# GLA score matmuls of a pair's two heads alternated in the two row groups of the array

## The chip, the cores and the metric

The kernel runs on one core of one Trainium2 chip. The metric is the device time of one execution in microseconds; a kernel's time is the median of its timed runs. The core has a matrix engine (TensorE, in the rows PE for its matmuls and PEld for its weight loads), VectorE (DVE), ScalarE (ACT), GpSimd (POOL) and SyncE (SP), which issues most of the loads. Each engine works through its own list of instructions in order.

## The reference, cut to what matters

The reference is one step of a diffusion trunk of two layers over 128 context tokens and 128 latent tokens, width 2048. Each layer has three mixers side by side (gated linear attention, softmax attention and DeltaNet) and an MLP. The change lies in the gated linear attention (GLA): 4 heads, key width 64, value width 128, run once forward and once backward over the tokens. Within a chunk its scores are

```python
b = jnp.cumsum(gc, axis=-2)
diff = b[..., :, None, :] - b[..., None, :, :]
dec = jnp.where(mask, jnp.exp(jnp.where(mask, diff, 0.0)), 0.0)
A = jnp.einsum('bhid,bhijd,bhjd->bhij', qc, dec, kc)
o = jnp.einsum('bhij,bhjv->bhiv', A, vc) + jnp.einsum('bhid,bhdv->bhiv', qc * jnp.exp(b), S)
```

so that each score is a sum over the 64 key channels of q, k and a decay between the two tokens, with the gate different in each channel.

## The kernel before, in words

All matmuls of the layers go through `mm` (line 85). Most of TensorE's work is a stream of projections and MLP products: a weight block is loaded by SyncE, split on ScalarE into a high part (`hi`) and on VectorE into a low part (`lo`), and multiplied with the activations (`g` and `gt` in the rows). `mod` are the products of the modulation.

The decay of GLA can't be pulled out of one product for all token pairs, so the kernel works in levels. For each level, a block size of 64, 32, 16, 8, 4, 2 or 1 tokens, queries and keys are scaled by the decay to the middle of their block (`scaled`: tiles `tq` and `tk_`, seven levels each). One product of 128 by 128 per level gives the scores of token pairs whose halves differ at that level, and a mask picks them. An eighth product, of the unscaled q and k, gives the diagonal. A token group `g` (0 context, 1 latent) and a column `c` hold a pair of heads: the tile has 128 partitions, the first head in partitions 0 to 63 and the second in 64 to 127. There are 4 pairs per layer and 8 in the kernel.

`intra(g, c, hh)` makes the scores of one head. It contracts over 64 partitions only, and `tile_position=(64 * hh, 0)` places the product in the upper or the lower half of the array's rows. The eight products go to two PSUM banks of the pool `pm` (three banks, used by the other steps of this chain too; `ga` in the rows): the diagonal and three levels in the first, four levels in the second, each bank with an order token of its own, so that within a bank the products are issued in this order. The diagonal is copied to the tile `AT` by ScalarE with a factor of 2, and then VectorE copies the seven levels into `AT` under their masks (COPY_PREDICATED in the rows). A bank can be given to a new tile when the last of its readers is done. `outs` multiplies `AT` with the values (`obg`).

`gla_chain` is a generator: it yields between its steps (decay, scaling, the scores of the first head, of the second, outs, stats). `weave` runs this chain, the two softmax chains (`att_chain`) and a normalisation together with a filler, which holds the remaining projections of the layer and the modulation. It keeps a clock of TensorE's assumed time; when no chain is due yet, it takes a piece of the filler. A chain is due again after `K0 + K1 *` the assumed time of its VectorE and ScalarE work (0.4 and 0.7). From the order that results, the framework's scheduler then fixes each engine's list at build time with a simulated timeline, and may move instructions against each other where data and order tokens allow.

The lines that the rows name: 85 is `mm`, 94 `tp`, 55 every VectorE and ScalarE instruction.

Of the kernel before, what the change touches and what calls it, by code (L numbers as in the profile page):

```python
# [12 lines left out]
I32 = mybir.dt.int32  # L13
AF = mybir.ActivationFunctionType
# [26 lines left out]
def tile_hybrid_step(ctx: ExitStack, tc: tile.TileContext, A: dict, O: dict):  # L41
# [17 lines left out]
    ve, se = Timed(nc.vector, 1 / 960, 0.13), Timed(nc.scalar, 1 / 1400, 0.27)  # L59

    def pool(name, bufs=1, **kw):
        return tc.tile_pool(name=name, bufs=bufs, **kw)
# [10 lines left out]
    pm = ctx.enter_context(pool("pm", 3, space=PS))  # L73
# [6 lines left out]
    def newtok():  # L80
        ntok[0] += 1
        return f"tok{ntok[0]}"

    def mm(out, lhsT, rhs, start=True, stop=True, tok=None, **kw):
        i = nc.tensor.matmul(out, lhsT=lhsT, rhs=rhs, start=start, stop=stop, **kw)  # L85
        n = math.prod(rhs.shape[1:])
        pe_t[0] += max(n / 2400 * (1 if rhs.dtype == F32R else 4), 0.027)
        if tok is not None:
            tc.stamp_issue_order_token(i.ins, tok)
        return i  # L90
# [21 lines left out]
    gmask = cp.tile([P, 7, P], F32, tag="c_gmask", name="gmask")  # L112
# [526 lines left out]
    for l in range(L):  # L639
        modc, s12, _, _ = mods[l]  # L640
# [23 lines left out]
        if l > 0:  # L664
            lay = open_layer(l)
        lctx, dnc, reg, sml, o_dn, gqk, gv, aq, akv, misc, dqk, vt = [
            lay[k] for k in ("lctx", "dnc", "reg", "sml", "o_dn", "gqk", "gv", "aq", "akv", "misc", "dqk", "vt")
        ]
# [184 lines left out]
        def pbank(nm, pp):  # L853
            t = pp.tile([P, 512], F32, tag="m", name=nm)
            return t.rearrange("p (h c) -> p h c", h=4)
# [39 lines left out]
        def dn_group(g):  # L895
            pp = (pm, pn)[g]

            def tr(nm, tag="tr", bufs=3):
                return dp.tile([P, 4, P], F32, tag=f"{tag}{g}", name=nm, bufs=bufs)
# [104 lines left out]
            for d in range(2):  # L1004
                yield
                vsrc = vt[:, g].rearrange("p (h v) -> p h v", h=4)
                if g == 1:
                    kb = bank("kb")
                    for h in range(4):
                        mm(kb[:, h], dqk[:, 4 + h, gs], s0d[:, d, h])  # L1010
                    R = tr("R")
                    for h in range(4):
                        ve.scalar_tensor_tensor(
                            R[:, h], kb[:, h], nec[:, d * 4 + h : d * 4 + h + 1], vsrc[:, h], ALU.mult, ALU.add
                        )
                else:
                    R = vsrc
                if g == 1:
                    yield
                vb = bank("vb")  # L1020
                for h in range(4):
                    mm(vb[:, h], N[d][:, h], R[:, h])
                v_ = tr("vn", "vn", 2)
# [80 lines left out]
        def gla_chain():  # L1104
# [4 lines left out]
            tq = gp.tile([P, 7, P], F32, tag="tq", name="tq")  # L1109
            tk_ = gp.tile([P, 7, P], F32, tag="tk", name="tk")  # L1110
            qi = gp.tile([P, 2, 2, P], F32, tag="qi", name="qi")
            ks = gp.tile([P, 2, 2, P], F32, tag="ks", name="ks")
            AT = gp.tile([P, 8, P], F32, tag="AT", name="AT")

            def decay(g, c, d):
                if c == 0 and d == 0:
                    lah = gp.tile([P, 512], F32R, tag="lah", name="lah")
                    lal = gp.tile([P, 512], F32R, tag="lal", name="lal")
                    se.activation(lah, t12[:, g], AF.Copy, scale=1.0 / 16.0)
                    ve.scalar_tensor_tensor(lal, t12[:, g], 1.0 / 16.0, lah.bitcast(F32), ALU.mult, ALU.subtract)  # L1120
                    lahl[:] = [lah, lal]
                lah, lal = lahl
                off = 0 if g == 0 else P
                e = gp.tile([P, 8, P], F32, tag="e", name="e", bufs=2)
                for b2 in range(2):
                    eb = pm.tile([P, 512], F32, tag="m", name="eb")
                    ls = slice(d * 256 + c * P, d * 256 + c * P + P)
                    rs_ = wr[d][:, off + b2 * 512 : off + b2 * 512 + 512]
                    mm(eb, lah[:, ls], rs_, start=True, stop=False)
                    mm(eb, lal[:, ls], rs_, start=False, stop=True)  # L1130
                    se.activation(e[:, 4 * b2 : 4 * b2 + 4].rearrange("p a b -> p (a b)"), eb, AF.Exp)
                return e

            def scaled(g, c, d, e):
                lb = 1 if g == 0 else 0
                q_ = gqk[:, c, g * P : g * P + P]
                k_ = gqk[:, 2 + c, g * P : g * P + P]
                for li, s in enumerate(GLEV):
                    ev = e[:, lb + li].rearrange("p (b h s) -> p b h s", h=2, s=s)
                    qv = q_.rearrange("p (b h s) -> p b h s", h=2, s=s)  # L1140
                    kv = k_.rearrange("p (b h s) -> p b h s", h=2, s=s)
                    tqv = tq[:, li].rearrange("p (b h s) -> p b h s", h=2, s=s)
                    tkv = tk_[:, li].rearrange("p (b h s) -> p b h s", h=2, s=s)
                    ve.tensor_tensor(tqv[:, :, 1 - d], qv[:, :, 1 - d], ev[:, :, 1 - d], ALU.mult)
                    ve.tensor_tensor(tkv[:, :, d], kv[:, :, d], ev[:, :, d], ALU.mult)
                if g == 0:
                    ve.tensor_tensor(ks[:, d, c], k_, e[:, 0], ALU.mult)
                else:
                    ve.tensor_tensor(qi[:, d, c], q_, e[:, 7], ALU.mult)

            def intra(g, c, hh):
                R = slice(64 * hh, 64 * hh + 64)
                i8 = g * 4 + c * 2 + hh
                tk0, tk1 = newtok(), newtok()
                b0 = pbank("ga0", pm)
                b1 = pbank("ga1", pm)
                gsl = slice(g * P, g * P + P)
                mm(b0[:, 0], gqk[R, 2 + c, gsl], gqk[R, c, gsl], tok=tk0, tile_position=(64 * hh, 0))
                for li in range(7):
                    o_ = (b0 if li < 3 else b1)[:, (li + 1) % 4]  # L1160
                    tt = tk0 if li < 3 else tk1
                    mm(o_, tk_[R, li], tq[R, li], tok=tt, tile_position=(64 * hh, 0))
                se.activation(AT[:, i8], b0[:, 0], AF.Copy, scale=2.0)
                for li in range(7):
                    src = (b0 if li < 3 else b1)[:, (li + 1) % 4]
                    ve.copy_predicated(AT[:, i8], gmask[:, li].bitcast(I32), src)

            def outs(g):
                gs = slice(g * P, g * P + P)
                ob = pbank("obg", pm)  # L1170
                tk = newtok()
                for h in range(4):
                    mm(ob[:, h], gv[:, g, h * P : h * P + P], AT[:, g * 4 + h], start=True, stop=(g == 0), tok=tk)
                    if g == 1:
                        for d in range(2):
                            mm(ob[:, h], s0g[0][:, d, h], qi[:, d, h // 2], start=False, stop=(d == 1), tok=tk)
                se.activation(o_gl[:, :, gs], ob, AF.Copy)
                sq = gp.tile([P, 4, P], F32, tag="tr", name="gsq", bufs=2)
                se.activation(sq, ob, AF.Square)
                return sq  # L1180

            def stats(g, sq):
                sb_ = pm.tile([P, 512], F32, tag="m", name="stgb")
                for h in range(4):
                    mm(sb_[:, h : h + 1], sq[:, h], ones[:, 0:1])
                ve.tensor_copy(stg[0].rearrange("p (h g) -> p h g", g=2)[:, :, g], sb_[:, 0:4])
# [4 lines left out]
            for i, (g, c, d) in enumerate(steps):  # L1191
                yield
                if i < 7:
                    es[i + 1] = decay(*steps[i + 1])
                    if i == 4:
                        s0g.append(rgl.tile([P, 2, 4, P], F32, tag="t12", name="s0g"))
                        nc.gpsimd.dma_start(s0g[0], A["s0_gla"][l])
                    yield
                scaled(g, c, d, es.pop(i))
                if d == 1:  # L1200
                    for hh in range(2):
                        yield
                        intra(g, c, hh)
                    if c == 1:
                        yield
                        sq = outs(g)
                        yield
                        stats(g, sq)
# [144 lines left out]
        wo = A["w_out"][l]  # L1353
        oatt = [att_chain(0), att_chain(1)]
        weave([gla_chain(), out_norm(ap, o_dn, sto, "od", TB, lay["rs16"][:, 0:8], pn)] + oatt, filler)
        while "end" not in marks:
            next(filler, None)
# [283 lines left out]
```

## Time and profile before

| | |
|---|---|
| time, median of 3 runs | 2603.95 us (2598.66 to 2604.85) |
| span of the profiled execution, first to last instruction | 2594.0 us |
| instructions in it | 47700 |
| TensorE matmul busy | 2526.2 us, 97% |
| VectorE busy | 1804.8 us, 70% |
| ScalarE busy | 1225.7 us, 47% |
| loaded from HBM | 602.41 MB |

The profiled execution is shown by its span; the page has no time for what lies before the first and after the last instruction. Matmul records overlap, since matmuls are pipelined: a record's length is not the time that it takes from the stream. That time is read from one record's start to the next one's. An fp32 product appears as two passes, that is two weight loads and two matmuls.

### The profile page before, as it was taken

To read this page: it belongs to the slowest core of one execution; us is meant where nothing else is said; L and a number is where in the kernel's file an instruction comes from. 1 tells how busy PE (TensorE), PEld (TensorE's weight loads), DVE (VectorE), ACT (ScalarE), POOL (GpSimd) and SP (SyncE) were. 2 spreads that over 40 slices of the span, in tenths; PEclk is the share of its full clock that TensorE was granted. 3 is DMA by queue.
4 is the path that set the end of the run, shared out by engine and by line. 5 is a ranking of instruction groups with operands and counts; after the bars stand their busy time and mean duration, and the time that the engine had idled before them with its cause. 6 is when DMAs were issued, how large, how long until landed. Compare 5 with 4: busy or idle time off the path is not lost. (4 is left out here: it accounts for less than half of the span.)

```text
span 2594.0 us, 47700 instructions
## 1 busy us (share of the span) xinstructions
PE 2526.2 (97%) x18988; PEld 2257.6 (87%) x18988; DVE 1804.8 (70%) x3197; ACT 1225.7 (47%) x1925; POOL 98.2 (4%) x121
## 2 busy tenths in 40 slices
PE   6999999999999999999999999999999999999999
PEld 4777678699988999999999888898999989999888
DVE  4457758558878767776766776786789865564665
ACT  3356244446454354344355653455565435445433
POOL 1000000003000000000002100000210000000000
PEclk9999999999999999999999999999999999999999
DMA  9966767776888877888876764435578766565664
GB/s 361 330 246 215 270 217 253 274 262 199 313 300 303 292 268 266 281 292 288 279 246 227 255 217 123 144 119 169 170 229 304 259 187 188 187 190 186 185 198 142
DMA packets 169551, 611.83 MB, mean 236 GB/s; under 512 B 19744, under 2 KB 20320, under 8 KB 169328
## 3 DMA queue, kind: packets, MB, share of 16 engines
q1 hardware_dynamic: 165024, 598.94, 68.3%
q0 software_dynamic: 2432, 6.61, 0.7%
q8 instruction: 149, 2.44, 0.4%
q10 hardware_dynamic: 1872, 3.23, 0.4%
q14 instruction: 74, 0.61, 0.1%
HBM read 602.41 MB, written 6.29 MB: 235 GB/s over the span
## 5 line engine op out<-in xcount | busy, mean ns | idle before, releaser
L55 ACT ACTIVATE hi<-raw 128x1024 fp32r<-128x1024 f32 (+1 forms) x742 | 784.4, 1057 | 1080.7 <-PE g L85 574.6
L55 DVE TENSOR_TENSOR lo<-raw,hi 128x1024 fp32r<-128x1024 f32 (+1 forms) x742 | 899.2, 1218 | 342.2 <-ACT hi L55 324.9
L85 PE MATMUL g<-act,hi 128*128 128x256 f32 (+1 forms) x7488 | 1055.5, 291 | 17.2 <-ACT hi L55 6.2
L85 PEld LDWEIGHTS g<-act,hi 128*128 128x128 f32 x7488 | 954.2, 189 | 98.5 <-issue 28.9
L85 PE MATMUL g<-act,lo 128*128 128x256 f32 x4000 | 561.3, 282 | 5.6 <-DVE lo L55 5.3
L85 PEld LDWEIGHTS g<-act,lo 128*128 128x128 f32 x4000 | 513.6, 189 | 19.6 <-DVE lo L55 9.5
L55 DVE SCALAR_TENSOR_TENSOR acc<-raw,sc,acc 128x1024 f32<-128x1024 f32 x240 | 299.1, 1280 | 130.6 <-DMA raw<-w_mod 128.0
L85 PE MATMUL g<-hid,hi 128*128 128x256 f32 (+1 forms) x1536 | 262.4, 319 | 2.1 <-DVE x L55 2.1
L55 DVE SCALAR_TENSOR_TENSOR x<-g,modc,x 128x128 f32<-128x128 f32 x448 | 142.0, 347 | 170.5 <-PE g L85 165.9
L85 PEld LDWEIGHTS g<-hid,hi 128*128 128x128 f32 x1536 | 217.2, 188 | 28.2 <-ACT hi L55 5.0
L85 PE MATMUL mod<-raw,sc 128*32 128x512 f32 (+1 forms) x1280 | 154.7, 526 | 20.5 <-DMA raw<-w_mod 18.7
L85 PE MATMUL gt<-hi,act 128*128 128x512 f32 x512 | 141.6, 409 | 3.3 <-ACT hi L55 3.3
L85 PE MATMUL g<-hid,lo 128*128 128x256 f32 x1024 | 142.1, 281 | 0.0
L85 PEld LDWEIGHTS g<-hid,lo 128*128 128x128 f32 x1024 | 134.7, 188 | 6.3 <-issue 0.8
L85 PEld LDWEIGHTS gt<-hi,act 128*128 128x128 f32 x512 | 93.9, 190 | 39.5 <-issue 11.3
L492 POOL TENSOR_TENSOR ht<-x,rstd 128x256 f32<-128x256 f32 x48 | 55.6, 1177 | 1011.5 <-ACT rstd L55 1008.1
L85 PEld LDWEIGHTS mod<-raw,sc 128*32 128x32 f32 x1280 | 30.9, 109 | 59.6 <-issue 13.8
L85 PE MATMUL gt<-lo,act 128*128 128x512 f32 x256 | 75.7, 403 | 0.0
L85 PE MATMUL gl<-hid,hi 128*128 128x258 f32 x384 | 70.4, 285 | 2.1 <-ACT hi L55 2.1
L85 PEld LDWEIGHTS gl<-hid,hi 128*128 128x128 f32 x384 | 59.3, 189 | 2.6 <-ACT hi L55 2.5
L85 PEld LDWEIGHTS gt<-lo,act 128*128 128x128 f32 x256 | 47.2, 188 | 12.6 <-issue 1.1
L85 PE MATMUL gl<-hid,lo 128*128 128x258 f32 x192 | 54.1, 284 | 0.7 <-DVE lo L55 0.6
(353 smaller groups left out, 1919.3 us busy)
## 6 DMA issues: line engine op xcount, KB each, us to landing
raw<-w_ff SPq DMA_DIRECT2D x512, 512.0 KB, 4.5
raw<-w_mod SPq DMA_DIRECT2D x384, 512.0 KB, 5.2
raw<-w_in SPq DMA_DIRECT2D x86, 512.0 KB, 4.2
raw<-w_tok SPq DMA_DIRECT2D x64, 512.0 KB, 4.4
raw<-w_out SPq DMA_DIRECT2D x64, 512.0 KB, 4.1
raw<-w_in SPq DMA_DIRECT2D x16, 448.0 KB, 6.1
x<-xT SPq DMA_DIRECT2D x8, 512.0 KB, 7.3
spill<-x ACTq DMA_DIRECT2D x4, 512.0 KB, 4.2
```

The source lines that it names most:

```text
L55: return f(out, *a, **kw)
L85: i = nc.tensor.matmul(out, lhsT=lhsT, rhs=rhs, start=start, stop=stop, **kw)
L492: nc.gpsimd.tensor_tensor(t, X["x"][:, k, :], rstd, ALU.mult)
```

## The change

`intra` now takes a pair of heads. It works in two parts of four products per head: first the diagonal and levels 0 to 2, then levels 3 to 6. In a part each head has a bank of its own, and the products of the two heads alternate level by level under one order token: first head in the upper rows, second head in the lower rows, next level. After a part's products come the copies of both heads, and then a `yield`; the caller yields once ahead of the first part. The number of products, their shapes and the copies stay as they are. Before, a head's eight products were written one after the other, with a `yield` ahead of each head; there are now three of them per pair (one ahead, one behind each part) in place of two.

```diff
@@ -1148,22 +1148,27 @@
                 else:
                     ve.tensor_tensor(qi[:, d, c], q_, e[:, 7], ALU.mult)
 
-            def intra(g, c, hh):
-                R = slice(64 * hh, 64 * hh + 64)
-                i8 = g * 4 + c * 2 + hh
-                tk0, tk1 = newtok(), newtok()
-                b0 = pbank("ga0", pm)
-                b1 = pbank("ga1", pm)
+            def intra(g, c):
                 gsl = slice(g * P, g * P + P)
-                mm(b0[:, 0], gqk[R, 2 + c, gsl], gqk[R, c, gsl], tok=tk0, tile_position=(64 * hh, 0))
-                for li in range(7):
-                    o_ = (b0 if li < 3 else b1)[:, (li + 1) % 4]
-                    tt = tk0 if li < 3 else tk1
-                    mm(o_, tk_[R, li], tq[R, li], tok=tt, tile_position=(64 * hh, 0))
-                se.activation(AT[:, i8], b0[:, 0], AF.Copy, scale=2.0)
-                for li in range(7):
-                    src = (b0 if li < 3 else b1)[:, (li + 1) % 4]
-                    ve.copy_predicated(AT[:, i8], gmask[:, li].bitcast(I32), src)
+                i8 = g * 4 + c * 2
+                rows = [slice(64 * hh, 64 * hh + 64) for hh in range(2)]
+                for part in range(2):
+                    banks = [pbank(f"ga{part}", pm) for _ in range(2)]
+                    tk = newtok()
+                    for b in range(4):
+                        li = 4 * part + b - 1
+                        for hh, R in enumerate(rows):
+                            if li < 0:
+                                kk, qq = gqk[R, 2 + c, gsl], gqk[R, c, gsl]
+                            else:
+                                kk, qq = tk_[R, li], tq[R, li]
+                            mm(banks[hh][:, b], kk, qq, tok=tk, tile_position=(64 * hh, 0))
+                    for hh in range(2):
+                        if part == 0:
+                            se.activation(AT[:, i8 + hh], banks[hh][:, 0], AF.Copy, scale=2.0)
+                        for b in range(1 if part == 0 else 0, 4):
+                            ve.copy_predicated(AT[:, i8 + hh], gmask[:, 4 * part + b - 1].bitcast(I32), banks[hh][:, b])
+                    yield
 
             def outs(g):
                 gs = slice(g * P, g * P + P)
@@ -1198,9 +1203,8 @@
                     yield
                 scaled(g, c, d, es.pop(i))
                 if d == 1:
-                    for hh in range(2):
-                        yield
-                        intra(g, c, hh)
+                    yield
+                    yield from intra(g, c)
                     if c == 1:
                         yield
                         sq = outs(g)
```

## Rows read from the trace of the kernel before

**Rows 1.** The page's part 1: busy us, share of the span, instructions.

```profile
PE 2526.2 (97%) x18988; PEld 2257.6 (87%) x18988; DVE 1804.8 (70%) x3197; ACT 1225.7 (47%) x1925; POOL 98.2 (4%) x121
```

**Rows 2.** Waits of TensorE, whole span: us in total, times, longest us.

```profile
PE mod L85 <- DMA raw<-w_mod: 18.7, 8, 12.6
...
```

**Rows 3.** The same in 365 to 500 us, and in 1640 to 1775 us.

```profile
PE g L85 <- DVE x L55: 1.2, 1, 1.2
...
PE ptb L94 <- DVE p L55: 3.0, 1, 3.0
...
```

**Rows 4.** By window: length, busy of PE, PEld, DVE, ACT, POOL, clock, DMA share, GB/s.

```profile
365.00:500.00 135.00, 133.84 (x938) 96.78 (x937) 101.14 (x335) 59.93 (x116) 4.34 (x8) 1.00 0.73 255
1640.00:1775.00 135.00, 129.73 (x889) 113.45 (x887) 105.64 (x325) 67.55 (x122) 3.82 (x7) 0.99 0.38 123
390.00:410.00 20.00, 20.00 (x160) 16.26 (x159) 19.76 (x63) 7.04 (x13) 1.65 (x3) 1.00 0.80 291
1684.00:1711.00 27.00, 27.00 (x224) 26.15 (x223) 27.00 (x86) 14.47 (x25) 0.55 (x1) 1.00 0.40 122
1711.00:1730.00 19.00, 19.00 (x146) 17.36 (x144) 13.21 (x46) 9.02 (x15) 0.00 (x0) 1.00 0.45 143
```

**Rows 5.** Instructions on tile ga, whole span: ns min/median/max, first and last start.

```profile
L85 PE MATMUL ga<-tq,tk x224: 272/272/373, 371.9 to 1732.4; 64*128 64x128 f32 x112
...
L55 DVE COPY_PREDICATED AT<-gmask,ga x112: 270/296/311, 375.3 to 1737.4; 128x128 f32<-128x128 int32 x112
...
L85 PE MATMUL ga<-gqk x32: 272/322/373, 371.5 to 1730.8; 64*128 64x128 f32 x32
```

**Rows 6.** Timeline of TensorE (start us, us, instruction), bursts of one head.

```profile
371.54 0.48 PE L85 MATMUL ga<-gqk 64*128 64x128 f32 x2
...
381.81 1.33 PE L85 MATMUL g<-act,hi 128*128 128x256 f32 x10
383.07 1.16 PE L85 MATMUL ga<-tq,tk 64*128 64x128 f32 x8
384.15 0.51 PE L85 MATMUL eb<-wr,lah 128*128 128x512 f32 x1
384.50 0.39 PE L85 MATMUL eb<-wr,lal 128*128 128x512 f32 x1
...
1730.62 0.48 PE L85 MATMUL ga<-gqk 64*128 64x128 f32 x2
1730.95 1.72 PE L85 MATMUL ga<-tq,tk 64*128 64x128 f32 x14
```

**Rows 7.** Timeline of TensorE, 459 to 461.2 us.

```profile
459.84 0.37 PE L85 MATMUL ga<-tq,tk 64*128 64x128 f32 x1
459.85 0.37 PE L85 MATMUL ga<-gqk 64*128 64x128 f32 x1
460.05 0.27 PE L85 MATMUL ga<-tq,tk 64*128 64x128 f32 x1
460.06 0.27 PE L85 MATMUL ga<-gqk 64*128 64x128 f32 x1
460.16 0.84 PE L85 MATMUL ga<-tq,tk 64*128 64x128 f32 x8
460.93 0.51 PE L85 MATMUL g<-act,hi 128*128 128x256 f32 x2
```

**Rows 8.** Timeline of TensorE, 434 to 446 us.

```profile
437.05 0.71 PE L85 MATMUL ga<-tq,tk 64*128 64x128 f32 x4
```

**Rows 9.** Timeline of ScalarE and VectorE, the first and fourth readers of a bank.

```profile
372.74 0.28 ACT L55 ACTIVATE AT<-ga 128x128 f32<-128x128 f32 x1 [0.67 <-PE ga L85]
...
378.15 0.29 DVE L55 COPY_PREDICATED AT<-gmask,ga 128x128 f32<-128x128 int32 x1
```

**Rows 10.** Timeline of VectorE; in brackets idle us before it and its releaser.

```profile
486.37 0.69 DVE L55 TENSOR_TENSOR o_gl<-o_gl,bcb 128x512 f32<-128x512 f32 x1 [3.45 <-PE bcb L85]
...
1729.75 0.30 DVE L55 COPY_PREDICATED AT<-gmask,ga 128x128 f32<-128x128 int32 x1 [3.13 <-PE ga L85]
```

## The prediction, made before the change was run

> **What bounds the kernel now.** I read the page's busy line first: TensorE's matmuls are busy for 97% of the span, VectorE 70%, ScalarE 47% [rows 1]. A busy matmul row does not prove that the engine never waits, so the second view is the list of waits, for TensorE alone. Over the whole kernel its largest entry is 18.7 us, for weights of the modulation [rows 2]. In the two stretches of the change (the gated linear attention, one per layer, 365 to 500 us and 1640 to 1775 us) the list has one entry in the first, 1.2 us, and in the second 3.0 us for the softmax's p and three entries of under 1 us, all at the stretches' ends [rows 3]. So TensorE's instruction stream is what sets the end there: other matmuls (the filler) stand between the attention's own steps and cover their latency. The third view is the table by window: VectorE has 101 us of work in the first 135 us and 106 in the second, but between 1684 and 1711 us it has no idle time left (27.00 of 27.00), and between 390 and 410 us hardly any (19.76 of 20); right behind the second of these it is idle for 5.8 of 19 us [rows 4]. The transfers take 0.73 and 0.38 of the DMA engines' time there. The granted clock is 1.00 and 0.99 there, that is the 2.4 GHz level [rows 4].
>
> **What the score matmuls cost now.** There are 256 passes in the trace (224 of the levels and 32 of the unscaled pair): 128 matmuls, two passes each [rows 5]. In a burst of one head passes follow each other every 0.1115 us: 14 of them take 1.72 us, less the 0.27 of the last, over 13 gaps [rows 6]. Each burst also pays for going from the full array to half of its rows and back. In the burst at 383.07 the g passes before it run every 0.117 us ((1.33 - 0.28) / 9), the last of them starts at 382.86, and the first score pass 0.21 later: 0.09 lost. The first two passes of a burst are 0.21 apart (0.48 - 0.27), 0.10 more than later ones. The last pass starts at 383.96 and what follows 0.20 later: 0.09. And that one's first record is 0.51 long where the next has 0.39: 0.11 or 0.12, I take 0.11. Together 0.39 us per burst [rows 6]. I count 28 bursts, 16 in the first layer and 12 in the second; the first is that at 371.54, the last that of 16 passes from 1730.62 [rows 6].
>
> Seven of the 28 already hold what the change wants: passes of both heads side by side. In the clearest both heads start together, at 459.84 and 459.85, go on at 460.05 and 460.06, and stay side by side until one runs out [rows 7]. That burst has 12 passes, four of them beside another, and lasts 1.09 us to the next matmul, where 12 in a row would need 0.21 + 10 x 0.1115 + 0.20 = 1.53: four passes cost nothing. Six bursts hide three passes each and one hides four, 22 in all. So the work now is (256 - 22) x 0.1115 + 28 x 0.39 = 26.1 + 10.9 = 37.0 us of TensorE.
>
> **The change part by part.** *Alternation.* A part has four levels of both heads, 16 passes, with an order token that keeps them alternating and a bank for each head, as the burst of [rows 7] has. If the heads run beside each other a part lasts as long as 8 passes of one: 8 x 0.1115 + 0.39 = 1.28 us. Eight pairs of two parts, each whole, are 16 x 1.28 = 20.5 us, a saving of 16.5. Every further break costs 0.39. Now a pair makes three bursts (8, 16 and 8 passes) where nothing breaks them, 24, and four more come from places like 437.05, where two levels run alone between other matmuls [rows 8]. I keep these four: 20 bursts, 22.1 us, a saving of 14.9. The bounds are 16.5 (16 bursts) and 11.8 (28 again, 8 x 0.39 more than 20).
>
> By the Trainium skill, TensorE: Matmul & The Clock Gate, section "Wait — 56ns, not 53.3ns?", the sequencer can need about 62 ns for each matmul and is the bound where the array needs less; two heads side by side ask for one pass every 56 ns. The rows at 459.84 hold the faster pace for eight passes only [rows 7], and no row shows it for 16. By that rule a part's 16 passes would take 0.99 us where I have 0.89, an estimate of 1.6 us more over 16 parts.
>
> *What VectorE and ScalarE do.* 112 masked copies as before [rows 5], and 16 scaled ones, of the same sizes; only their order changes (three and three, then four and four). Cost nothing, since the work is equal.
>
> *The banks.* The pool has three. Part 1 needs two, and the second of these is the first head's bank of part 0, free after one ScalarE copy and three masked copies. Before, the same release held back only the last 8 of a pair's 32 passes; now it holds back 16. What is queued behind the first matmul of part 1 on TensorE is the filler, if the planner puts it there. At the first pair the bank is read from 372.74 to 378.44 [rows 9], and the passes that wait for it run at 383.07, 0.21 behind filler that had been put in between [rows 6]. I take nothing for it; the other end is a rival below. The attention's chain itself gets longer by the four masked copies that now follow the last part, about 4 x 0.29 = 1.2 us per pair. At the first layer's end VectorE, done with its own step of this chain, has stood 3.45 us until TensorE came to the next [rows 10], so 1.2 us later costs nothing; at the second's the stretch ends with the softmax chain, whose p TensorE waits for [rows 3], not with this one.
>
> *One more step.* The generator yields once more per pair; the planner may put one more piece of filler there. It is work that has to run anyway: nothing, as long as filler is left.
>
> *What does not arrive.* Where VectorE has no idle time, TensorE cannot get ahead for good. The bursts inside the full windows are those at 1697.87 and 1699.21 (24 passes, three of them beside others: 21 x 0.1115 + 2 x 0.39 = 3.1 us, afterwards a part and a half, 1.9) and two of the same kind at 394.0 and 397.5. I give up the 1.2 us of each, 2.4 together. Ends: 0 (VectorE's 5.8 idle us behind the second window take it back) and 8.6 (the whole of the second layer's half, 7.4, and the first's 1.2).
>
> Sum: 14.9 - 2.4 = 12.5 us less. The profiled span is 2594.0 us, and 2581.5 is expected for it. The page gives no time around it; the median of the runs, 2603.95, lies 9.95 above the span, and I leave that as it is: 2603.95 - 12.5 = 2591.5 us. A change of 0.3%, 7.8 us, is what can be told from none. If every part is whole and nothing is lost it is 2587.5.
>
> **The rivals.**
> *VectorE sets the pace (no change).* The second layer's half is lost, and the first layer's loses 1.2: 7.4 - 1.2 = 6.2, so 2597.8. For it: the full window, and TensorE's wait for p at the stretch's end. Against it: at 1729.75 VectorE itself has stood 3.13 us for score matmuls [rows 10], so it had caught up before the last bursts.
>
> *Parts broken up (no change).* If the levels come one by one, as at 435.88, each pair of matmuls is a burst of its own: 2 x 0.1115 + 0.39 = 0.61 us for one level of both heads. With half of the parts so, 8 x 1.28 + 32 x 0.61 = 29.8 us, a saving of 7.2, less 2.4: 2599.2. For it: four breaks now. Against it: 22 of the 28 bursts have 6 passes or more.
>
> *The row groups do not run together (no change).* Then 256 passes in a row and 20 bursts: 28.5 + 7.8 = 36.3, 0.7 less than now: 2603.3. The rows at 459.84 speak against it.
>
> *TensorE stands for the bank (slower).* If part 1 is queued right behind part 0, with no filler between, TensorE stands until the first head's bank has been read. At the first pair its reading takes from 372.74 to 378.44, 5.7 us, because the masked copies wait in VectorE's queue behind other work [rows 9]. With half of that, 2.85 us in each of 8 pairs, 22.8 us come on top: 2603.95 - 12.5 + 22.8 = 2614.3. It decides from 12.5 / 8 = 1.6 us per pair. For it: 16 passes behind that wait and not 8, and an order that is fixed before the run. Against it: the wait exists now and costs TensorE nothing [rows 3].
>
> **How the numbers follow.** Forecast 0.66, VectorE's pace 0.11, broken parts 0.10, no overlap 0.03, bank 0.10. The forecast's own range is 2586 to 2596: 16.5 less at one end, 11.8 - 2.4 = 9.4 at the other, and 1.6 us on either side for the order of everything else, which the planner works out anew (an estimate, half of the 3.0 us that is its largest wait in the stretches now [rows 3], rounded up). The range to the other cases is 2585 to 2604: it takes in all but the bank rival and a little at either end. Faster by over 0.3% (below 2596.1): 0.62 of the forecast's 0.66, a third of VectorE's pace and a fifth of the broken parts, 0.68. Slower by over 0.3%: 0.09 from the bank rival and 0.01 for an order that falls out badly, 0.10. The rest, 0.22, is within 0.3%.
>
> **What would show it.** After: 256 score passes in about 20 bursts, 16 at least; a part of 16 passes 0.9 us from its first start to its last, two starts within 0.02 us of each other every 0.11; the time from 365 us to the end of each layer's stretch shorter by 5 to 8 us and everything behind it unchanged. The forecast is wrong if TensorE's waits list a score matmul behind an AT copy (bank), if its waits for lo or hi in the two stretches grow by more than 3 us (VectorE), or if starts within a part are 0.11 apart one by one (no overlap).

## The result, and the profile after

The kernel with the change takes 2591.5 us (median of 8 runs, 2584.8 to 2598.9) where the kernel before took 2604.4 beside it on the same chip (8 runs, 2598.7 to 2609.5): a ratio of 0.9943, 95% interval 0.9928 to 0.9958, or 15 us less (11 to 19; the two medians lie 12.9 apart). Run again beside other kernels it gave 0.9929 (0.9913 to 0.9945) and a median of 2585.0. The forecast was 2591.5 us, with a range of 2585 to 2604.

The two profiled executions can't be compared by their spans. After's is 2597.0 us, the longest of its eight runs (2598.9 us, 1.9 more than the span; 1.8 to 2.2 in the other runs). Before's, 2594.0 plus 1.9, was faster than all of the eight runs above. What hides the gain between them lies where TensorE's order is the same in both: from the end of the first layer's stretch (below) to the start of the second's it is 1046.5 us in before's profile, 1059.6 in after's and 1047.3 in a second profile of the kernel with the change (e2). Most of it is one piece of the first layer's MLP: 274.2, 283.1 and 276.7 us. So the comparison goes by stretch: from a layer's first `eb<-wr,lah` product to the first `gl<-hid` product of its MLP.

The table by window, for the first layer's stretch and the second's (columns as in rows 4; the length is the first number). The kernel before:

```profile
359.30:588.20 228.90, 227.74 (x1703) 182.53 (x1702) 156.27 (x443) 105.80 (x190) 4.34 (x8) 1.00 0.75 260
1634.70:1854.20 219.50, 214.23 (x1581) 196.60 (x1581) 165.25 (x447) 115.51 (x200) 3.82 (x7) 0.99 0.47 151
```

The kernel with the change:

```profile
362.20:587.70 225.50, 224.62 (x1704) 178.16 (x1703) 156.49 (x448) 105.53 (x190) 4.33 (x8) 1.00 0.76 264
1647.30:1856.90 209.60, 207.17 (x1581) 190.68 (x1580) 163.35 (x447) 115.00 (x200) 3.81 (x7) 1.00 0.51 158
```

The first layer's stretch is 3.4 us shorter, the second's 9.9: 13.3 together. These lengths repeat within 2 us where TensorE's order is the same. The second layer's is 219.5, 219.8 and 219.3 in three profiles that have before's order there, and 209.6, 209.6, 209.6, 209.8 and 211.4 in five that have after's; the first layer's is 229.0 and 230.3, and 225.5, 226.4 and 226.9. (The means differ by 3.4 and 9.5.)

The page's busy line after [rows 1] and the first entry of TensorE's waits [rows 2] show no other bound:

```profile
PE 2522.5 (97%) x18988; PEld 2252.9 (87%) x18988; DVE 1802.7 (69%) x3197; ACT 1225.5 (47%) x1925; POOL 98.3 (4%) x121
```

```profile
PE mod L85 <- DMA raw<-w_mod: 18.0, 8, 12.9
```

The instructions on tile ga are as many and as long as before [rows 5]:

```profile
L85 PE MATMUL ga<-tq,tk x224: 272/272/374, 375.7 to 1741.6; 64*128 64x128 f32 x112
...
L55 DVE COPY_PREDICATED AT<-gmask,ga x112: 274/297/308, 380.4 to 1749.2; 128x128 f32<-128x128 int32 x112
```

What is new is how they stand. The timeline of TensorE at the first pair (start us, us, instruction; the rows of a burst overlap where the two heads run side by side) answers to rows 6 and 7:

```profile
374.51 0.48 PE L85 MATMUL ga<-gqk 64*128 64x128 f32 x2
374.93 0.73 PE L85 MATMUL g<-act,hi 128*128 128x256 f32 x4
375.50 0.28 PE L85 MATMUL g<-act,lo 128*128 128x256 f32 x1
375.71 0.37 PE L85 MATMUL ga<-gqk 64*128 64x128 f32 x1
375.71 0.37 PE L85 MATMUL ga<-tq,tk 64*128 64x128 f32 x1
375.92 0.27 PE L85 MATMUL ga<-gqk 64*128 64x128 f32 x1
375.93 0.94 PE L85 MATMUL ga<-tq,tk 64*128 64x128 f32 x13
376.80 1.08 PE L85 MATMUL g<-act,lo 128*128 128x256 f32 x7
```

A burst is a run of score passes with no other product between them; a pass is hidden when it starts within 0.02 us of one of the other head. Here are sixteen passes from 375.71 to the last start at 376.60 (375.93 + 0.94 - 0.27): 0.89 us, eight of them hidden. But the first head's diagonal (two passes, 374.51) has gone out alone: the order that was fixed at build time puts five other products between it and its partner, which follows 1.2 us later beside the first head's first level. Why is not settled; a bank that comes free later for the second head would do it, but no run here tests that. Most pairs come as 2, 16 and 14 passes: the lone product, then the rest of part 0 with the first product of part 1, then the rest of part 1. In the whole trace I count 24 bursts and 110 hidden passes, so by the prediction's prices (256 - 110) x 0.1115 + 24 x 0.39 = 25.6 us of score work, where before by the same count has 37.0. Added up from starts, it is 25.57 where before has 37.05: 11.5 less, 5.8 in the first layer and 5.7 in the second (some tenths more or less by how the edges of a burst are counted).

TensorE's waits in the second layer's stretch (1652.5 to 1787.5 us), which answer to rows 3:

```profile
PE g L85 <- DVE x L55: 1.5, 1, 1.5
...
```

No score matmul and no `AT` copy appears there, and the wait of `ptb` for p is gone. Its place on TensorE shows what that was worth. Timeline of the kernel before (idle us and releaser in brackets):

```profile
1759.98 1.94 PE L94 MATMUL ptb<-c_ident,p 128*128 128x128 f32 x8 [2.98 <-DVE p L55]
1761.75 1.89 PE L85 MATMUL oatb<-pT,cvv 128*128 128x512 f32 x2
1763.48 1.02 PE L85 MATMUL oatb<-pT,akv 128*128 128x512 f32 x2
```

The same instructions after:

```profile
1763.49 1.04 PE L94 MATMUL ptb<-c_ident,p 128*128 128x128 f32 x8
1764.77 1.12 PE L85 MATMUL oatb<-pT,cvv 128*128 128x512 f32 x2 [0.25 <-ACT pT L55]
1765.73 1.02 PE L85 MATMUL oatb<-pT,akv 128*128 128x512 f32 x2
```

Before, TensorE stood 2.98 us, and the rows behind the wait took 3.50 us (1759.98 to 1763.48) where after they take 2.24. The window of these 3.5 us before has a granted clock of 0.51, the 1.2 GHz level; the same rows after run at 1.00 (before, then after):

```profile
1759.90:1763.40 3.50, 3.42 (x10) 2.40 (x11) 1.14 (x2) 1.19 (x2) 0.00 (x0) 0.51 0.55 207
```

```profile
1763.40:1766.60 3.20, 2.95 (x16) 1.75 (x15) 3.09 (x4) 1.52 (x3) 0.97 (x2) 1.00 0.65 184
```

The second layer's 9.9 us are thus 5.7 of score work, 3.0 of waiting and 1.3 of lower clock. In the first layer 5.8 of score work give 3.4.

### The profile page after: what moved, and what is told of

Its sections match the earlier page's. It is cut to its first block, busy times and chain, and to the rows that moved or that the text cites. A ratio compares the mean times of both kernels' runs of the same rounds, so it can differ in the third digit from the quotient of the medians.

```text
span 2597.0 us, 47711 instructions
## 1 busy us (share of the span) xinstructions
PE 2522.5 (97%) x18988; PEld 2252.9 (87%) x18988; DVE 1802.7 (69%) x3197; ACT 1225.5 (47%) x1925; POOL 98.3 (4%) x121
## 5 line engine op out<-in xcount | busy, mean ns | idle before, releaser
L85 PEld LDWEIGHTS g<-act,hi 128*128 128x128 f32 x7488 | 955.4, 189 | 101.0 <-ACT hi L55 27.4
L85 PEld LDWEIGHTS g<-act,lo 128*128 128x128 f32 x4000 | 514.1, 189 | 24.1 <-DVE lo L55 11.8
```

## The experiments

Each was timed in five rounds; ratios are to the kernel before on the same chip. "Stretches" are the first and the second layer's, from one profile each. Score work is added up from starts; passes that are not hidden x 0.1115 + bursts x 0.39 gives the same within 0.4 us, in e7 within 1.1.

| kernel | us | ratio (95%) | stretches, us | score us (bursts) |
|---|---|---|---|---|
| before | 2602 to 2605 | 1 | 229.0, 219.5 | 37.05 (28) |
| after | 2591.5 | 0.9943 (0.9928 to 0.9958) | 225.5, 209.6 | 25.57 (24) |
| e2 after again | 2585.0 | 0.9929 (0.9913 to 0.9945) | 226.4, 209.6 | 25.57 (24) |
| e1 head by head | 2609.8 | 1.0022 (1.0010 to 1.0034) | 234.1, 222.9 | 36.56 (28) |
| e3 after, scores twice | 2612.2 | 1.0029 (1.0017 to 1.0042) | 242.0, 222.1 | 39.61 (23) |
| e4 before, scores twice | 2637.1 | 1.0130 (1.0113 to 1.0148) | 256.4, 230.4 | 62.28 (20) |
| e5 after, mod token | 2590.9 | 0.9944 (0.9925 to 0.9963) | 227.9, 209.6 | 26.00 (24) |
| e6 before, mod token | 2613.0 | 1.0031 (1.0014 to 1.0048) | 234.7, 219.8 | 38.28 (29) |
| e7 head by head, mod token | 2609.1 | 1.0020 (1.0005 to 1.0034) | 232.6, 223.0 | 39.01 (31) |
| e8 one yield less | 2589.5 | 0.9946 (0.9930 to 0.9963) | 229.7, 211.4 | 25.04 (23) |
| e9 before, fewer copies | 2620.2 | 1.0055 (1.0034 to 1.0077) | 244.9, 221.7 | 38.00 (30) |
| e10 after, fewer copies | 2589.9 | 0.9945 (0.9927 to 0.9963) | 224.8, 214.9 | 25.67 (24) |
| e11 first layer only | 2599.9 | 0.9985 (0.9972 to 0.9998) | 226.9, 219.3 | 31.24 (25) |
| e12 second layer only | 2594.1 | 0.9961 (0.9945 to 0.9977) | 230.3, 209.8 | 31.38 (27) |

**e1, the alternation undone.** Parts, banks and yields stay; only the loop order within a part goes back.

```diff
-                    for b in range(4):
-                        li = 4 * part + b - 1
-                        for hh, R in enumerate(rows):
+                    for hh, R in enumerate(rows):
+                        for b in range(4):
+                            li = 4 * part + b - 1
```

> The new kernel with the alternation alone undone: same parts, banks, copies and yields, but within a part the first head's four products are written ahead of the second head's four. In TensorE's order this makes 28 bursts, and the heads meet in nine places, at three passes each. Theory (the gain is TensorE time saved by the overlap): (256 - 27) x 0.1115 + 28 x 0.39 = 36.5 us of score work against 37.0 before and 25.6 in the new kernel, so the time of the kernel before within 2 us, 2602 to 2606, some 11 us slower than the new kernel. Rival (the gain comes from the new parts, banks and yields, through the plan of everything else): as fast as the new kernel, 2590 to 2593.

The score work is as expected (36.56 us), the time is 5.7 us above before, not equal to it. So the parts, banks and yields without the alternation give no gain; the gain comes with the alternation and the order of everything else that the planner makes with it. That the heads stand in different row groups does not suffice. The timeline of e1's first burst shows where one head's four products meet the other's: the second head's diagonal (`gqk`) starts among the last passes of the first, and only those run side by side:

```profile
373.51 0.49 PE L85 MATMUL ga<-tq,tk 64*128 64x128 f32 x3
373.74 0.37 PE L85 MATMUL ga<-gqk 64*128 64x128 f32 x1
373.85 0.27 PE L85 MATMUL ga<-tq,tk 64*128 64x128 f32 x1
373.95 0.27 PE L85 MATMUL ga<-gqk 64*128 64x128 f32 x1
```

The wait for p is there, at 4.1 us, and the modulation's products in the first layer's stretch are issued in 38 pieces (runs with no other product between them) in place of 33. The 5.7 us led to e5 to e7.

**e2, the kernel with the change once more** (no edit).

> The new kernel once more, unchanged, for another profiled execution. Both theories: 2588 to 2594. In the profiled execution of the new kernel the first layer's MLP between 1073 and 1358 us took 8.9 us longer than before, with the same order of TensorE's instructions. Theory (chance of that execution): here that piece is within 3 us of the kernel before. Rival (the changed stretch moves the loads of what follows and the MLP pays): 7 to 10 us longer again.

The stretches repeat within 1 us; the MLP piece that was 8.9 us longer in after's first profile is 2.45 longer here. That difference belongs to the execution, not to the change. The median, 2585.0 us, lies below the 2588 to 2594 that both theories had.

**e3 and e4, each score product issued twice** (the second into the same place, so nothing else changes in the data).

```diff
+                        t_ = pe_t[0]
+                        for hh, R in enumerate(rows):
...
+                            mm(banks[hh][:, b], kk, qq, tok=tk, tile_position=(64 * hh, 0))
+                        pe_t[0] = t_
```

> The new kernel with each pair of products of a level issued twice, alternating, the second time over the first (same results, copies and waits; the planner's clock does not count the second). 256 passes more. Theory (heads run side by side, and each us of TensorE in these stretches is a us of time): 128 x 0.1115 = 14.3 us more, less one burst, 0.4: 2591.5 + 13.9 = 2605.4. Rival (VectorE sets part of the pace, so that a part of TensorE's time there is hidden): 5 to 9 us more, 2596 to 2600. If the heads did not run side by side in the longer bursts: 28 us more, 2619.

> The kernel before with each product issued twice in a row, head by head (same results, copies and waits; the planner's clock does not count the second). 256 passes more, 20 bursts in TensorE's order where there were 28. Theory: 256 x 0.1115 = 28.5 more, less 8 x 0.39 = 3.1: 25.4 us more, 2604.4 + 25.4 = 2629.8. Rival (VectorE's pace hides a part): 10 to 17 us more, 2614 to 2621.

The prices of the score work hold: 14.04 us more of it in e3 and 25.2 in e4. A burst of e3 holds 32 passes, from 375.46 to the last start at 377.25, 1.79 us:

```profile
375.46 0.60 PE L85 MATMUL ga<-gqk 64*128 64x128 f32 x5
375.80 0.27 PE L85 MATMUL ga<-tq,tk 64*128 64x128 f32 x1
375.90 0.27 PE L85 MATMUL ga<-gqk 64*128 64x128 f32 x1
375.91 1.61 PE L85 MATMUL ga<-tq,tk 64*128 64x128 f32 x25
```

The times miss both expectations: they rise by more, 21 us in e3 (27 against e2, which was timed beside it) where the theory had 13.9, and 34 in e4 where it had 25.4. In the first layer's stretch e3 has 16.5 us more for 6.4 of score work, e4 27.4 for 11.3. The rest stands above all in two groups of products that are the same in number but issued in more pieces. From each start to the next one, the modulation takes 35.6 us in before (33 pieces), 36.7 after (34), 44.6 in e3 (42) and 47.8 in e4 (45); the `g` products take 141.8, 143.4, 146.4 and 146.4.

In the second layer e4's stretch grows by 10.9 us only, for 13.9 of score work: TensorE comes later to the place where before has the wait for p [rows 3], and that wait is gone, without any alternation. Its list of waits there has for `ptb` only

```profile
PE ptb L94 <- ACT hi L55: 0.3, 1, 0.3
```

So about 3 us of the doubled work are hidden there, as much as the wait was long; nothing shows that VectorE hides more.

**e5, e6 and e7, the modulation's products kept together.** The four products of one block of input channels share an order token, the half whose weights come last first.

```diff
-            for gg in range(4):
+            tok = newtok()
+            for gg in (2, 3, 0, 1):
...
+                    tok=tok,
```

> New kernel, and in the modulation the four products of one block of input channels (its four column groups) get one order token, the half whose weights come last first, so that they are issued together. The order that was fixed at build time has 125 bursts of these products in place of 134, and 24 bursts of score passes as before. Theory (a group that is issued in two pieces costs TensorE about 1 us more than one that is issued whole, and this is what carries the differences between kernels beyond the score passes; from the modulation's 35.6 us in 33 bursts to 47.8 us in 45 in the first layer's stretch): 9 bursts fewer are 9 us, so about 2582 us, 0.8% below the kernel before. Rival (broken groups cost nothing; the extra time of the earlier kernels went along with something else): 2591, as the new kernel. Second rival (holding a group until its last weights are there makes TensorE wait at the start of the layers): over 2596, and longer waits of mod for the DMA than 18.0 us.

> Kernel before with the same order token on the modulation's groups: 127 bursts of modulation products in place of 133, 29 bursts of score passes. Theory: 6 us less than the kernel before, 2598; and against the new kernel with the same token, whose modulation is then as whole as this one's, the alternation is worth its score passes and the 2 bursts: 37.5 - 25.6 + 2 = 14 us, about 2596 to 2598. Rival (broken groups cost nothing): 2604, as the kernel before.

> New kernel with the alternation undone (in each part the first head's four products, then the second's) and the modulation's order token: 127 bursts of modulation products in place of the 138 that the same kernel had without the token, 31 bursts of score passes. Theory: the 5.7 us by which the kernel without the alternation came out slower than the kernel before were broken modulation groups; with the token it is equal to the kernel before with the token within 3 us (score passes 37 to 38 us, 127 bursts in both), so 2598, and 11 us less than without the token. Rival (the parts themselves cost it: two banks held by one step, masked copies later): still 5 to 6 us slower than the kernel before with the token.

The times do not follow the theory: e5 stays at 2590.9 us where it had 2582 and the rival 2591, e6 and e7 come to 2613.0 and 2609.1 where it had 2598. The modulation does get cheaper; its TensorE row over the first layer's stretch, after and then e5 (34 pieces, 28 pieces):

```profile
362.20:587.70 225.50, 40.47 (x240) 7.83 (x240) 0.36 (x2) 1.21 (x2) 1.00 0.76 264
```

```profile
359.30:587.20 227.90, 35.31 (x244) 7.33 (x240) 0.37 (x2) 1.18 (x2) 0.99 0.76 265
```

Counted from starts it is 3.6 us less, 0.6 for each piece saved, but the time stays where it was, and before with the token is 8 us slower than without it. In e5 the same stretch holds 15 `g` passes more, which the new order takes in from ahead of it (about 1.8 us, an estimate at the 0.117 us of [rows 6]), and it has new waits elsewhere:

```profile
PE g L85 <- DVE x L55: 2.1, 1, 2.1
PE g L85 <- ACT hi L55: 1.5, 2, 0.9
PE oatb L85 <- ACT pT L55: 1.3, 1, 1.3
```

So keeping the groups whole doesn't make the kernel faster. That first stretches with more pieces are longer (e1, e3, e4, e9) is what the rows show; that the pieces are the cause isn't shown. The three runs do show something else: from e7 to e5 only the loop order differs, as from e1 to after. The medians differ by 18.3 us in both pairs, and by 24.8 between e1 and e2, which were timed beside each other. (e7 came out 4 us below e6, where the theory had them equal and the rival had e7 above.)

**e8, without the yield behind the second part.**

```diff
-                    yield
+                    if part == 0:
+                        yield
```

> New kernel without the second yield of intra (the one behind the second part of a pair), so that the chain goes on from the last copies to its next step without a turn for the filler in between: two yields per pair, as before the change. 23 bursts of score passes, 136 of the modulation in place of 134. Theory (one more yield costs nothing as long as filler is left; the time moves with bursts): 2591 + 2 - 0.4, within 3 us of the new kernel. Rival (the extra yield delays the chain by a piece of filler per pair): 5 us or more below the new kernel, under 2587.

As the theory said: the extra yield costs nothing that can be measured.

**e9 and e10, four masked copies per head in place of seven.** Both leave the scores of three levels out of `AT`, so they compute something else than the reference; they serve for the times alone. The edit of e9 (e10 picks the same levels within its parts):

```diff
-                for li in range(7):
+                for li in (0, 2, 3, 6):
```

> Kernel before without the masked copies of the second, fifth and sixth level: four copies per head in place of seven, 24 copies or 7.1 us of VectorE less per layer (the scores of these levels are computed and left out of AT). All 128 score matmuls stay. Theory (in the second layer's stretch VectorE reaches the last p late: TensorE, there after as many other products in the kernel before, the new one and the one without alternation, waits for it, and pays a stretch at the lower clock behind the wait; the new kernel's gain beyond its score passes in that layer comes from being rid of that): with 7.1 us less on VectorE the wait of ptb for p is gone or under 0.5 us (before: 3.0), and the second layer's stretch is 4 to 6 us shorter than before's 219.5, though its score passes stay at 18 us. The first layer's stretch has no such wait: it moves only with its order (141 bursts of modulation products in place of 133). Rival (VectorE has no part in it; the wait falls out by the order): the wait stays at 3 us and the stretch at 219 to 220.

> New kernel without the same masked copies, 7.1 us of VectorE less per layer; 24 bursts of score passes, 133 of the modulation (134 in the new kernel). Theory (in the new kernel p comes before TensorE wants it, so VectorE sets no end): the second layer's stretch stays within 1.5 us of 209.6 and the first's within 2.5 of 226, the time within 4 us of the new kernel's 2591.5. Rival (VectorE's pace still takes a part of the score saving, as the 2.4 us given up in the prediction): both stretches together 4 us or more shorter, under 2587.

Both theories on the second layer miss. In e9 the wait is as the rival had it, 3.1 us, though the stretch is 221.7 and not 219 to 220: with 7.1 us less to do VectorE is as late with p as it was. In e10 the time and the first layer's stretch are within what the theory allowed, but the second's is 214.9 where it had 209.6: the alternation is untouched and the wait is back (timeline of TensorE in e10; then the clock behind it):

```profile
1754.19 1.06 PE L94 MATMUL ptb<-c_ident,p 128*128 128x128 f32 x8 [2.69 <-DVE p L55]
1755.50 1.66 PE L85 MATMUL oatb<-pT,cvv 128*128 128x512 f32 x2 [0.25 <-ACT pT L55]
```

```profile
1755.40:1760.30 4.90, 4.80 (x7) 2.01 (x8) 0.22 (x1) 1.90 (x6) 0.00 (x0) 0.65 0.05 19
```

The cause is in VectorE's list just ahead of p. Its timeline in the kernel before:

```profile
1755.15 1.22 DVE L55 TENSOR_REDUCE sm<-p 128x4 f32<-128x1024 f32 x1 [0.57 <-ACT p L55]
1756.29 1.21 DVE L55 TENSOR_TENSOR lo<-raw,hi 128x1024 fp32r<-128x1024 f32 x1
1757.42 0.17 DVE L55 RECIPROCAL sm<-sm 128x4 f32<-128x4 f32 x1
1757.51 1.19 DVE L55 TENSOR_TENSOR lo<-raw,hi 128x1024 fp32r<-128x1024 f32 x1
1758.62 1.22 DVE L55 TENSOR_TENSOR p<-p,sm 128x1024 f32<-128x1024 f32 x1
```

In the kernel with the change:

```profile
1760.29 1.22 DVE L55 TENSOR_REDUCE sm<-p 128x4 f32<-128x1024 f32 x1
...
1761.54 0.18 DVE L55 RECIPROCAL sm<-sm 128x4 f32<-128x4 f32 x1
...
1761.75 1.22 DVE L55 TENSOR_TENSOR p<-p,sm 128x1024 f32<-128x1024 f32 x1
1762.93 2.36 DVE L55 TENSOR_TENSOR lo<-raw,hi 128x1024 fp32r<-128x1024 f32 x2
```

In e10:

```profile
1748.83 1.23 DVE L55 TENSOR_TENSOR lo<-raw,hi 128x1024 fp32r<-128x1024 f32 x1 [0.64 <-ACT hi L55]
1749.97 1.21 DVE L55 TENSOR_REDUCE sm<-p 128x4 f32<-128x1024 f32 x1
1751.22 0.18 DVE L55 RECIPROCAL sm<-sm 128x4 f32<-128x4 f32 x1
1751.68 1.23 DVE L55 TENSOR_TENSOR lo<-raw,hi 128x1024 fp32r<-128x1024 f32 x1 [0.29 <-ACT hi L55]
1752.83 1.22 DVE L55 TENSOR_TENSOR p<-p,sm 128x1024 f32<-128x1024 f32 x1
```

Before, two weight splits stand between the sum and p, 2.2 us of the 3.0, and VectorE itself stands 0.57 us for ScalarE just ahead of them; in e10 one split stands there and one ahead of the sum, with 0.9 us of waiting for ScalarE ahead of the two; e9 has the two of before. After, both splits come behind p, and the sum starts 3.20 us ahead of TensorE's getting to the transposes of p (1763.49), where before it started 1.85 ahead (1759.98 less the 2.98 of waiting). On TensorE the transposes of this p begin with the 717th pass of the stretch (scores not counted) in before, after, e1, e9 and e10 alike. So the 4.2 us that the second layer gains beyond its scores come with the place of two splits, and an earlier sum, in a list that was worked out anew. The list belongs to the build; in e10 the same alternation did not get it, and e4, head by head, is rid of the wait. That the alternation makes it likelier isn't shown.

In e9 the first layer's stretch grew by 16 us, with 41 pieces of the modulation and 75 of the `g` products (before: 33 and 56). How the planner's order comes to that was not followed up.

**e11 and e12, the change in one layer only.** The other layer has the code of before. The edit of e11 (e12 has `l == 1`):

```diff
-                    yield
-                    yield from intra(g, c)
+                    if l == 0:
+                        yield
+                        yield from intra(g, c)
+                    else:
+                        for hh in range(2):
+                            yield
+                            intra_head(g, c, hh)
```

> The pair-wise, alternating scores in the first layer alone; the second layer has the code of before. 25 bursts of score passes. Theory (the two layers' parts of the gain are apart: 3 us in the first layer, 10 in the second): first layer's stretch 225 to 227 us, the second's 219.5 with the wait for p of 3 us, time 2600 to 2602. Rival (both layers gain equally, 6 to 7 us): 2597 to 2598.

> The pair-wise, alternating scores in the second layer alone; the first layer has the code of before. 27 bursts of score passes. Theory: first layer's stretch 228 to 230 us, the second's 209.6 without a wait for p, time 2593 to 2595. Rival (both layers gain equally): 2597 to 2598.

The theory holds in both (2599.9 us where 2600 to 2602 was expected, and 2594.1): 0.15% and 0.39% below before, and each stretch has the length it has in the kernel whose code it shares. The parts add within their intervals: 3.9 + 10.2 us by the ratios (2.5 + 8.3 by the medians), each with 3 to 4 us of uncertainty either way, where the whole change gave 15 and, in e2, 18.5 by the ratios.

No version beat the kernel with the change beyond its interval. The four builds with the alternation in both layers and each product once (after, e5, e8, e10) lie at ratios of 0.9929 to 0.9946, the five without it (before, e1, e6, e7, e9) at 1 to 1.0055, so the gain is not the luck of one order.

## Why the prediction was right, and where it was so by two errors

- **The mechanism, and the price of a part: right.** 16 passes take 0.89 us from the first start to the last, the two starts of a pair 0.006 to 0.008 us apart. By the Trainium skill's rule that was weighed (TensorE: Matmul & The Clock Gate, section "Wait — 56ns, not 53.3ns?"), about 62 ns a matmul with hardware decode off, their 15 gaps would be 0.93 us, an estimate. The rows at 375.71 don't show that bound, and e3's 32 passes show it less: 1.79 us, where 31 gaps by that rule are 1.92. Whether hardware decode was on no row tells.
- **The number of bursts: wrong, the term that was mis-sized.** 20 bursts and a saving of 14.9 us were predicted, 11.8 at the least. It is 24 and 11.5, below the lower bound, because the bound counted breaks between whole parts only. Eight times one product of two passes goes out alone, which costs a burst and hides nothing: 4 bursts x 0.39 = 1.6 us, and 18 passes fewer hidden than the 128 of whole parts, 2.0 us. The prediction had no term for a product that the order parts from its partner, though the kernel before has such lone products too, as at 435.88. The Trainium skill (TensorEngine Tiling (Array Packing), section "Key Properties") says that changing the tiling mode drains the engine. The trace shows a loss at each change, 0.39 us for a burst; that a drain makes it no row shows.
- **"What does not arrive", 2.4 us lost to VectorE in its full windows: wrong place, and the right amount by chance.** 2.4 us were lost in the first layer (5.8 of score work, 3.4 of the stretch), but not by waiting: TensorE's waits there are 0.4 us for act and under that for others, 1.2 for hi in e2. The modulation has 1.0 to 2.0 us more, in 34 pieces, and `g` 1.6; some smaller groups have less.
- **The second layer's end: not foreseen.** The prediction took the wait for p [rows 3] as what the second stretch ends with and as a sign for VectorE's pace, and had no term for its going away. It went, with the lower clock behind it: 4.2 us.
- **The sum.** 11.5 - 2.4 + 4.2 = 13.3 us in the stretches, against 12.5 predicted and 15 (11 to 19) measured. The last 1.7 lie inside the interval. The agreement is partly luck: 3.4 too much for the scores and 4.2 not foreseen cancel. So is the median of 2591.5 us to the tenth, since the same kernel gave 2585.0 in e2.
- **The span's own time: wrong.** The 9.95 us taken as what lies around the span are 1.8 to 2.2 in the runs after; the rest was one short execution. Since the sum was made as a difference on the median, this did no harm.
- **The rivals.** VectorE's pace: after and e12 exclude it as it was put, since the second layer, whose half it would have cost, gains more than its score work. The wait for p is the part of it that is there: it hides about 3 us in e4. Broken parts: none of the parts is broken into single levels, but the lone products are a small case of it. No overlap: excluded by the rows at 375.71; e1 is what it would look like. TensorE standing for a bank: no such wait in the list.
- **What was to show it.** "Each stretch shorter by 5 to 8 us" did not hold for either layer (3.4 and 9.9), "everything behind it unchanged" held between the two stretches for TensorE's order but not for its time, and behind the second for the time (739.8 and 740.1 us to the end) but not wholly for the order.

What stays open is why the first layer's stretch gives back 2.4 us, and in other builds more (5 in e1, 16 in e9). The time stands in the modulation and `g`, cut into more pieces, as in e3 and e4. e5 shows that keeping the modulation's groups whole doesn't get it back.

## What to carry to other kernels

Here products of half the rows cost half only where their issue alternated between the row groups; placing them there was not enough. So price such a change by pairs and by bursts, and count the products that the order parts from their partner. When a planner works out the order anew, expect some us either way in each stretch, and compare stretches with their counts of pieces and their waits, since one profile's span says little: the same 8170 passes between the two stretches, in the same order on TensorE, took 1040.3 to 1059.6 us in the eleven profiles here that have that order. Where an engine waits for another, read the other's list right ahead of the awaited instruction before blaming its load: here two splits of 1.2 us each stood there, and 7 us less work changed nothing.

## What the runs showed of the hardware

- Two passes of 64 rows in different row groups start 0.006 to 0.008 us apart after the change, from the first pair on (0.003 to 0.014 in before and e1), and a pair takes 0.1115 us, as one pass does alone.
- Head by head the second row group comes in only for the last passes of the first: 3 of 16 hidden in a burst that holds eight of each head, and 3 of 48 in e4's first burst.
- Behind waits of 3.0 us in before, 2.7 in e10 the granted clock fell for some us (0.51 over 3.5 us, 0.65 over 4.9), that is to the 1.2 GHz level for most or part of them; in e10 the first 1.3 us behind the wait were still at 1.00. In before that makes the wait dearer by 1.3 us than its own length.
